# Rotation tables of an SSM on ScalarE, state tiles that stay, and four loads or uses moved by a few slots

## The chip, the cores and the metric

One core of a Trainium2 chip (trn2) runs the kernel. The metric is the device time of one execution in microseconds (us). Its engines: PE (TensorE; PEld is its weight load), DVE (VectorE), ACT (ScalarE), POOL (GpSimd) and SP, which issues most of the DMAs. Each engine takes its instructions in the order of the program, and waits for semaphores set by the others.

## The reference

One layer over x of 4096 rows and 1024 columns, in float32:

```
h    = rmsnorm(x) * pre_g
su, sg, pu, pg, q, k, v, ag = split(h @ W_in)        (widths 256 256 256 256 512 128 128 512)
y_ssm  = GLU(gelu(S5(su) + D*su)) * silu(sg)
y_pool = scale * GroupLinear(meanpool(pu) - pu) * silu(pg)
y_attn = windowed attention(q, k, v, sink) * silu(ag)
x + rmsnorm(concat(y_ssm, y_pool, y_attn) @ W_out) * post_g
```

S5 is a bidirectional complex diagonal recurrence: 16 groups of 16 channels, 64 complex states in each direction, h[t] = lambda * h[t-1] + B u[t], read out by C.

## The kernel before

**Stages.** A matmul in float32 precision is made of three: every operand is held as a high half (rounded by a copy on ScalarE) and a low half (the difference, made on DVE or POOL). The work goes in blocks of 512 rows (8 blocks) and chunks of 128 output columns. Stage 1 projects pool and SSM inputs, normalises x, splits it and stores the split x (`xd`); beside it DVE prepares the SSM's matrices and angle tables, one record of 689 columns for each group (`swd`). Stage 2 projects q, k, v and runs the attention. Stage 3, the gate stage (about 960 to 1300 us), projects the gates sg and ag (`p3_block`), and the 16 SSM groups run beside it (`ssm_group`, lines 1026 to 1110). The output stage multiplies by W_out and finishes.

**The order of the work.** It is written out by a clock of slots (`Slots`, lines 84 to 126): `e.at(slot, fn)` queues a function for a slot, `e.gen` runs a generator, whose `yield n` lets n slots pass, and `e.step()` emits everything that stands in the present slot, in the order in which it was queued there, and goes on to the next. A slot of the gate stage holds 6 projection matmuls, a chunk is four slots. A slot is no time: it fixes only in which order each engine, and SP, gets its instructions. `split(hi, lo, src, eng, lag)` (line 186) copies the high half on ScalarE now and puts the low half on `eng` one slot later.

**One SSM group.** The recurrence over 8 rows at a time is done by matrices, which leaves 512 steps for each group. They are turned into a real recurrence by a rotation: the drive (vr, vi) is multiplied by cos and sin of an angle table, scanned with a real decay rho, and turned back. A group starts every `SSM_PACE` = 8 slots. Its steps, by slot offset: 0 the loads of its record and of u; 4 the split of u (low half on POOL); 6 the angle table `ang`, a sum of two short tables, on POOL; 7 the split of its matrices `w`, and the reduction of the angles to half a turn on DVE (`kt`, `ang`, lines 1045 and 1046); 8 sin and cos on ScalarE (lines 1051 to 1053; cos by Abs and a second Sin); 10 to 12 three products on PE (`mm3`); 13 and 14 the rotation (DVE, and sums on POOL); 15 the split of `wc`; 16 and 17 four scans on DVE with two memsets ahead of each pair (a scan of the state tile's lower 64 partitions runs forward, one of the upper 64 backward); 18 the products that turn the states back: two with S on POOL, two with C on DVE; 20 their sums on POOL; 22 and 23 the splits of `hr` and `hi`; 26 and 27 the last matmuls (lines 1103 and 1105); 28 the copy of the result; 29 its store. So four groups are under way at once, and one engine sees offsets o, o+8, o+16, o+24 of four groups in the same slot.

**What else the change touches.** `p3_open` (line 1000) opens the gate stage: it loads rho, the post gains, the GLU's bias and the GLU's weights, and splits these at once (lag 0, lines 1015 to 1018). The gate chunks are taken out of PSUM on ScalarE, one slot after they are done (`ev_g`, activation in line 1147), and a chunk uses one of two banks. `load_wo` (line 1115) loads a half of a W_out matrix into one of three raw buffers and splits it two slots later. In stage 1, `x_split` (line 260) stores the split x to `xd` (line 279), and `sched_stats` (line 306) computes the row scales of a block two blocks ahead, stores them (`rb_store`) and loads them back, spread over all partitions (`rb_load`, line 335).

## Time and profile before

| | us |
|---|---|
| three runs: median (lowest to highest) | 1708.84 (1708.26 to 1712.75) |
| the profiled execution: its own time | 1709.39 |
| its span, first to last instruction | 1707.6 |
| PE busy in the span | 1592.8 (93%) |
| DVE busy | 1152.2 (67%) |
| ACT busy | 743.1 (44%) |
| POOL busy | 635.4 (37%) |
| mean granted TensorE clock | 0.967 of full speed |

The profile is one execution, read on the core. All times in it count from the start of the span. Matmuls are pipelined, so their busy time is more than the time they occupy PE for: they start 0.23 us apart at full clock and are shown as 0.39 us long. "Idle before" is the time in which an engine had nothing to do ahead of an instruction, with what ended it.

### The profile page before, as it was taken

Reading aid. Unit: us, or ns where it says so; the run is one execution under the profiler, and the core shown is the slowest. Engines: PE = TensorE matmul, PEld = TensorE weight load, DVE = VectorE, ACT = ScalarE, POOL = GpSimd, SP = SyncE. Lnnn points to the kernel's source line nnn. Section 1 sums busy time; section 2 is a strip of 40 time slices with the busy share of each in tenths; the row PEclk is TensorE's granted clock in tenths of the full one; section 3 lists DMA queues with packets and bytes.
Section 4 is the critical chain, followed back from the end, with each engine's and each line's share of the span. In section 5 each row is a group of like instructions: output and inputs, shape, how many; then the busy total and the mean of one; then the engine's idle time right before and its main releaser. Section 6 shows DMA issues by size and latency. Waiting matters only on the chain.

```text
span 1707.6 us, 21061 instructions
## 1 busy us (share of the span) xinstructions
PE 1592.8 (93%) x7364; PEld 1303.7 (76%) x7364; DVE 1152.2 (67%) x2183; ACT 743.1 (44%) x1608; POOL 635.4 (37%) x398
## 2 busy tenths in 40 slices
PE   7997789999999999999999988887889999999998
PEld 5776567778888888888888776666677788888886
DVE  6777768576777777777987378877884745444441
ACT  5323333236666666676776333232333332222221
POOL 0433334341233333333233065565561434334342
PEclk9999899999999999999999999999898999999999
DMA  7597798873221212222333543455358354554532
GB/s 232 183 246 196 195 243 245 315 240 131 87 92 63 69 63 96 83 69 81 119 110 112 200 147 111 159 171 164 104 174 252 121 183 157 164 172 149 163 131 77
DMA packets 121551, 259.07 MB, mean 152 GB/s; under 512 B 31458, under 2 KB 64994, under 8 KB 109668
## 3 DMA queue, kind: packets, MB, share of 16 engines
q1 hardware_dynamic: 115876, 243.03, 45.0%
q10 hardware_dynamic: 5568, 14.68, 2.6%
q8 instruction: 58, 0.95, 0.2%
q14 instruction: 49, 0.40, 0.1%
HBM read 168.93 MB, written 89.80 MB: 152 GB/s over the span
## 4 chain that ended last, share of the span: by engine, by line
PE 45%; DVE 21%; DMA 11%; issue 11%; POOL 9%; ACT 2%; SPq 1%; ACTq 0%; POOLq 0%; DVEq 0%
PE mm L349 5%; PE mm L350 5%; PE mm L351 5%; PE po L894 5%; PE tp L904 5%; PE mm L360 3%; PE o L1260 3%; PE o L1258 3%; PE o L1259 3%; DMA xs<-in_x_dram 3%; PE s L865 3%; PE s L864 3%; POOL ot L161 2%; DMA ga<-agate 2%; DVE xt L164 2%
## 5 line engine op out<-in xcount | busy, mean ns | idle before, releaser
L349 PE MATMUL mm<-xk,w 128*128 128x512 f32 x968 | 391.8, 405 | 8.4 <-ACT gg L1147 6.4
L350 PE MATMUL mm<-xk,w 128*128 128x512 f32 x968 | 386.1, 399 | 0.5 <-DVE xk L164 0.5
L351 PE MATMUL mm<-xk,w 128*128 128x512 f32 x968 | 384.7, 397 | 1.3 <-DVE w L161 1.3
L161 POOL TENSOR_TENSOR ns<-ns,es 128x1536 f32<-128x1536 f32 (+1 forms) x64 | 172.5, 2696 | 403.1 <-ACT pp L172 190.1
L349 PEld LDWEIGHTS mm<-xk,w 128*128 128x128 f32 x968 | 186.3, 192 | 45.4 <-ACT gg L1147 7.4
L351 PEld LDWEIGHTS mm<-xk,w 128*128 128x128 f32 x968 | 185.8, 192 | 43.9 <-DVE w L161 2.9
L350 PEld LDWEIGHTS mm<-xk,w 128*128 128x128 f32 x968 | 186.4, 193 | 35.3 <-DVE xk L164 1.6
L1258 PE MATMUL o<-wo,yk 128*128 128x512 f32 x512 | 201.2, 393 | 3.5 <-ACT gg L1147 3.1
L866 DVE CUSTOM_DVE_ANT_0 ns<-s,cst,nsink 128x384 f32<-128x384 f32 (+1 forms) x256 | 145.8, 607 | 84.6 <-PE s L865 83.4
L1260 PE MATMUL o<-wo,yk 128*128 128x512 f32 x512 | 201.5, 394 | 1.0 <-DVE yk L164 1.0
L1259 PE MATMUL o<-wo,yk 128*128 128x512 f32 x512 | 201.5, 394 | 0.0
L172 ACT ACTIVATE pp<-tp 128x512 fp32r<-128x512 f32 x188 | 112.3, 597 | 170.6 <-PE tp L904 169.6
L360 PE MATMUL mm<-xk,w 128*128 128x512 f32 x552 | 156.4, 422 | 24.3 <-DVE xk L161 14.1
L855 ACT ACTIVATE ns<-ns,nm 128x384 f32<-128x384 f32 (+1 forms) x256 | 152.3, 598 | 2.0 <-DVE nm L866 2.0
L360 PEld LDWEIGHTS mm<-xk,w 128*128 128x128 f32 x552 | 106.1, 200 | 56.0 <-DVE xk L161 18.8
L161 DVE TENSOR_TENSOR pp<-tp,pp 128x512 fp32r<-128x512 f32 x188 | 129.1, 687 | 18.6 <-ACT pp L172 17.2
L894 PE MATMUL po<-pp,vr 128*128 128x512 f32 x376 | 128.2, 422 | 0.0
L904 PE MATMUL tp<-cst,ns 128*128 128x128 f32 x752 | 112.7, 272 | 7.3 <-DVE pp L161 7.3
L904 PEld LDWEIGHTS tp<-cst,ns 128*128 128x128 f32 x752 | 93.1, 140 | 34.4 <-issue 10.1
L1258 PEld LDWEIGHTS o<-wo,yk 128*128 128x128 f32 x512 | 96.5, 189 | 26.3 <-ACT gg L1147 3.5
L1260 PEld LDWEIGHTS o<-wo,yk 128*128 128x128 f32 x512 | 96.6, 189 | 22.6 <-DVE yk L164 1.4
L1259 PEld LDWEIGHTS o<-wo,yk 128*128 128x128 f32 x512 | 96.4, 188 | 21.7
(312 smaller groups left out, 2706.4 us busy)
## 6 DMA issues: line engine op xcount, KB each, us to landing
xk<-xd SPq DMA_DIRECT2D x60, 1024.0 KB
xd<-xk SPq DMA_DIRECT2D x32, 1024.0 KB
xt<-in_xT_dram SPq DMA_DIRECT2D x35, 512.0 KB
xres<-in_x_dram SPq DMA_DIRECT2D x32, 512.0 KB
out_dram<-ot SPq DMA_DIRECT2D x31, 512.0 KB
xs<-in_x_dram ACTq DMA_DIRECT2D x24, 512.0 KB
raw<-in_w_in_dram SPq DMA_DIRECT2D x32, 256.0 KB
yattn<-ysb SPq DMA_DIRECT2D x32, 256.0 KB
```

The source lines that it names most:

```text
L161: return eng.tensor_tensor(out=out, in0=in0, in1=in1, op=op)
L349: T.matmul(o, lhsT=w[:, 0, k], rhs=xh, start=(k == 0), stop=False)
L350: T.matmul(o, lhsT=w[:, 0, k], rhs=xl, start=False, stop=False)
L351: T.matmul(o, lhsT=w[:, 1, k], rhs=xh, start=False, stop=(k == NK - 1))
L360: T.matmul(o, lhsT=w[:, i, k], rhs=XK[b, k][h], start=(n == 0), stop=(n == 3 * NK - 1))
L855: S.activation(out=ns[:, hh, :nk], in_=ns[:, hh, :nk], func=AF.Exp, scale=-1.0, bias=nm[:, hh:hh + 1], accum_out=su[:, hh:hh + 1])
L866: V.tensor_tensor_reduce(out=ns[:, hh, :nk], in0=sp_[:, :nk], in1=cst[:, C_D + c0:C_D + c0 + nk], scale=-(2.0 ** -(h + 1)), scalar=R["nsin ...
L894: T.matmul(po, lhsT=VR[:, (ta + kb) % 8, kv], rhs=pp[:, i], start=(kb == 0 and i == 0), stop=(kb == nkb - 1 and i == 1))
L904: T.transpose(tp[:, hh], ns[:, hh, kb * P:(kb + 1) * P], ident)
L1258: T.matmul(o, lhsT=y[:, 0, ts_], rhs=WO[kk][:, 0, hs], start=first, stop=False)
L1259: T.matmul(o, lhsT=y[:, 0, ts_], rhs=WO[kk][:, 1, hs], start=False, stop=False)
L1260: T.matmul(o, lhsT=y[:, 1, ts_], rhs=WO[kk][:, 0, hs], start=False, stop=last)
```

## The change

Seven edits. (1) In a group, the matrices `w` are split with u at offset 4 and not at 7. (2) The angles are no longer reduced on DVE. At offset 7 four activations make both tables in one tile `cs` of two halves: |a| for the cosine, |a - 1/4| for the sine, then over both halves | |.| - 1/2 |, and one Sin over both; the constant -1/4 gets a column of its own. `ang` moves from offset 6 to 5. (3) The state tiles are two that stay for the whole stage (`gs0`, `gs1`), whose zero columns are written once in `p3_open`. (4) The turning back is one product of both states with C on DVE, over 1024 columns, and one with S on POOL, which is written over the state tile; two sums follow as before. (5) The last matmuls of a group move from offsets 26 and 27 to 28 and 29. (6) The GLU's weights are loaded 30 slots later, one half after the other, each split five slots after its load (low half by one more slot). (7) The split of a W_out half follows its load by 4 slots instead of 2, the store of split x comes 2 slots later, and the load of the row scales 2 slots later.

```diff
--- before.py
+++ after.py
@@ -31,12 +31,11 @@
 CH_SU, CH_SG, CH_PU, CH_PG, CH_Q, CH_K, CH_V, CH_AG = 0, 2, 4, 6, 8, 12, 13, 14
 
 C_ID, C_D, C_E, C_CT, C_INVW, C_EDGE, C_QS = 0, 128, 512, 520, 568, 570, 602
-C_NHALF, C_E1, C_HPI, C_ONE = 606, 614, 742, 743
-NCST = 744
+C_NHALF, C_E1, C_HPI, C_ONE, C_NQ = 606, 614, 742, 743, 744
+NCST = 745
 REC = 689
 TWO_PI = 2.0 * math.pi
 TURN = 6.283185
-RND = 12582912.0
 
 
 def host_constants():
@@ -70,6 +69,7 @@
     c[:, C_E1:C_E1 + 128] = math.e
     c[:, C_HPI] = math.pi / 2
     c[:, C_ONE] = 1.0
+    c[:, C_NQ] = -0.25
     return c
 
 
@@ -276,7 +276,7 @@
             else:
                 tt(V, xk[:, 1, 0], xt[:, 0], f(xk[:, 0, 0]), ALU.subtract)
                 tt(PL, xk[:, 1, 1], xt[:, 1], f(xk[:, 0, 1]), ALU.subtract)
-                e.at(e.now + 6, lambda: dma(out=xd[b % NB, i], in_=f(xk.rearrange("p h j c -> p (h j c)"))))
+                e.at(e.now + 8, lambda: dma(out=xd[b % NB, i], in_=f(xk.rearrange("p h j c -> p (h j c)"))))
             have_x(b, i, xk)
 
         if lag:
@@ -332,7 +332,7 @@
         e.at(d0 + 18, mean, label="p1")
         e.at(d0 + 19, root, label="p1")
         e.at(d0 + 22, rb_store, b, label="p1")
-        e.at(d0 + 28, rb_load, b, label="main")
+        e.at(d0 + 30, rb_load, b, label="main")
 
     def rb_store(s):
         dma(out=rbd[s].rearrange("(j p) -> p j", p=P), in_=rstd[:, 4 * s:4 * s + 4])
@@ -1012,11 +1012,23 @@
         dma(out=glb[:, 0:4], in_=A["glu_b"])
         ts(glb[:, 4:6], glb[:, 2:4], 0.5, ALU.mult)
         gw = cw.tile([P, 2, 2, 4, P], F32R, name="gw")
-        for kk in range(2):
-            raw = wraw.tile([P, 4, P], F32, tag="raw", name="raw")
-            dma(out=raw.rearrange("p m c -> p (m c)"), in_=A["glu_w"][:, kk])
-            split(gw[:, 0, kk], gw[:, 1, kk], raw, V, 0)
-        return dict(ph=ph, sv=sv, gbc=gbc, glb=glb, gw=gw, rho=rho)
+
+        def glu_weights():
+            for kk in range(2):
+                raw = wraw.tile([P, 4, P], F32, tag="raw", name="raw")
+                dma(out=raw.rearrange("p m c -> p (m c)"), in_=A["glu_w"][:, kk])
+                yield 5
+                split(gw[:, 0, kk], gw[:, 1, kk], raw, V)
+
+        e.gen(e.now + 30, glu_weights(), label="main")
+
+        gs = []
+        for n in range(2):
+            gt = sv.tile([P, 2, NC], F32, name=f"gs{n}")
+            V.memset(gt[0:64, :, 0:1], 0.0)
+            V.memset(gt[64:128, :, NC - 1:NC], 0.0)
+            gs.append(gt)
+        return dict(ph=ph, sv=sv, gbc=gbc, glb=glb, gw=gw, rho=rho, gs=gs)
 
     def mm3(o, wh, wl, r, first, last):
         T.matmul(o, lhsT=wh, rhs=r[:, 0], start=first, stop=False)
@@ -1032,26 +1044,24 @@
         yield 4
         ur = sv.tile([P, 2, NC], F32R, tag="ur", name="ur", bufs=2)
         split(ur[:, 0], ur[:, 1], u, PL)
-        yield 2
+        w = sv.tile([P, 2, 3, P], F32R, tag="wb", name="wb", bufs=2)
+        split(w[:, 0], w[:, 1], rec[:, 0:384].rearrange("p (m c) -> p m c", m=3), V)
+        yield 1
+
 
         shc = [P, 16, 32]
         ang = sv.tile(shc, F32, tag="ang", name="ang")
         tt(PL, ang, bc(rec[:, 672:688].unsqueeze(2), shc), bc(rec[:, 640:672].unsqueeze(1), shc), ALU.add)
         rho = bc(R["rho"][:, g:g + 1], [P, NC])
-        yield 1
-        w = sv.tile([P, 2, 3, P], F32R, tag="wb", name="wb", bufs=2)
-        split(w[:, 0], w[:, 1], rec[:, 0:384].rearrange("p (m c) -> p m c", m=3), V)
-        kt = sv.tile(shc, F32, tag="kt", name="kt")
-        ts(kt, ang, RND, ALU.add)
-        stt(ang, kt, RND, ang, ALU.subtract, ALU.subtract)
-        yield 1
-        C_ = sv.tile([P, NC], F32, tag="ct", name="ct", bufs=2)
-        S_ = sv.tile([P, NC], F32, tag="st", name="st", bufs=2)
+        yield 2
+        cs = sv.tile([P, 2, NC], F32, tag="cs", name="cs", bufs=2)
         av = ang.rearrange("p a b -> p (a b)")
-        S.activation(out=S_, in_=av, func=AF.Sin, scale=-TURN)
-        S.activation(out=C_, in_=av, func=AF.Abs)
-        S.activation(out=C_, in_=C_, func=AF.Sin, scale=-TURN, bias=cst[:, C_HPI:C_HPI + 1])
-        yield 2
+        S.activation(out=cs[:, 0], in_=av, func=AF.Abs)
+        S.activation(out=cs[:, 1], in_=av, func=AF.Abs, bias=cst[:, C_NQ:C_NQ + 1])
+        S.activation(out=cs, in_=cs, func=AF.Abs, bias=cst[:, C_NHALF:C_NHALF + 1])
+        S.activation(out=cs, in_=cs, func=AF.Sin, scale=-TURN, bias=cst[:, C_HPI:C_HPI + 1])
+        C_, S_ = cs[:, 0], cs[:, 1]
+        yield 3
         vr = bank(4, [P, NC], "vr")
         mm3(vr, w[:, 0, 0], w[:, 1, 0], ur, True, True)
         yield 1
@@ -1061,45 +1071,39 @@
         o = bank((6, 7, 2, 3)[g % 4], [P, NC], "y")
         mm3(o, w[:, 0, 2], w[:, 1, 2], ur, True, False)
         yield 1
-        wr = sv.tile([P, NC], F32, tag="wr", name="wr", bufs=2)
-        wi = sv.tile([P, NC], F32, tag="wi", name="wi", bufs=2)
-        t2 = sv.tile([P, NC], F32, tag="t2", name="t2")
-        t3 = sv.tile([P, NC], F32, tag="t3", name="t3")
-        tt(V, wr, vr, C_, ALU.mult)
-        tt(V, t2, vi, S_, ALU.mult)
-        yield 1
-        tt(PL, wr, wr, t2, ALU.add)
-        tt(V, wi, vi, C_, ALU.mult)
-        tt(V, t3, vr, S_, ALU.mult)
-        yield 1
-        tt(PL, wi, wi, t3, ALU.subtract)
+        wt = sv.tile([P, 2, NC], F32, tag="wt", name="wt", bufs=2)
+        t2 = sv.tile([P, 2, NC], F32, tag="t2", name="t2")
+        tt(V, wt[:, 0], vr, C_, ALU.mult)
+        tt(V, t2[:, 0], vi, S_, ALU.mult)
+        yield 1
+        tt(PL, wt[:, 0], wt[:, 0], t2[:, 0], ALU.add)
+        tt(V, wt[:, 1], vi, C_, ALU.mult)
+        tt(V, t2[:, 1], vr, S_, ALU.mult)
+        yield 1
+        tt(PL, wt[:, 1], wt[:, 1], t2[:, 1], ALU.subtract)
         wc = sv.tile([P, 2, 2, P], F32R, tag="wc", name="wc", bufs=2)
         split(wc[:, 0], wc[:, 1], rec[:, 384:640].rearrange("p (m c) -> p m c", m=2), V)
         yield 1
-        gr = sv.tile([P, NC], F32, tag="gr", name="gr")
-        gi = sv.tile([P, NC], F32, tag="gi", name="gi")
-        for gt, wt in ((gr, wr), (gi, wi)):
-            V.memset(gt[0:64, 0:1], 0.0)
-            V.memset(gt[64:128, NC - 1:NC], 0.0)
-            V.tensor_tensor_scan(out=gt[0:64, 1:NC], data0=rho[0:64, 0:NC - 1], data1=wt[0:64, 0:NC - 1],
+        gs = R["gs"][g % 2]
+        for i in range(2):
+            V.tensor_tensor_scan(out=gs[0:64, i, 1:NC], data0=rho[0:64, 0:NC - 1], data1=wt[0:64, i, 0:NC - 1],
                                  initial=0.0, op0=ALU.mult, op1=ALU.add)
-            V.tensor_tensor_scan(out=gt[64:128, NC - 2::-1], data0=rho[64:128, 0:NC - 1],
-                                 data1=wt[64:128, NC - 1:0:-1], initial=0.0, op0=ALU.mult, op1=ALU.add)
+            V.tensor_tensor_scan(out=gs[64:128, i, NC - 2::-1], data0=rho[64:128, 0:NC - 1],
+                                 data1=wt[64:128, i, NC - 1:0:-1], initial=0.0, op0=ALU.mult, op1=ALU.add)
             yield 1
-        tt(PL, t2, gi, S_, ALU.mult)
-        tt(PL, wi, gr, S_, ALU.mult)
-        tt(V, wr, gr, C_, ALU.mult)
-        tt(V, t3, gi, C_, ALU.mult)
+        sh2 = [P, 2, NC]
+        tt(V, wt, gs, bc(C_.unsqueeze(1), sh2), ALU.mult)
+        tt(PL, gs, gs, bc(S_.unsqueeze(1), sh2), ALU.mult)
         yield 2
-        tt(PL, wr, wr, t2, ALU.subtract)
-        tt(PL, wi, wi, t3, ALU.add)
+        tt(PL, wt[:, 0], wt[:, 0], gs[:, 1], ALU.subtract)
+        tt(PL, wt[:, 1], wt[:, 1], gs[:, 0], ALU.add)
         yield 2
         hr = sv.tile([P, 2, NC], F32R, tag="hr", name="hr")
-        split(hr[:, 0], hr[:, 1], wr, V)
+        split(hr[:, 0], hr[:, 1], wt[:, 0], V)
         yield 1
         hi = sv.tile([P, 2, NC], F32R, tag="hi", name="hi")
-        split(hi[:, 0], hi[:, 1], wi, V)
-        yield 3
+        split(hi[:, 0], hi[:, 1], wt[:, 1], V)
+        yield 5
         mm3(o, wc[:, 0, 0], wc[:, 1, 0], hr, False, False)
         yield 1
         mm3(o, wc[:, 0, 1], wc[:, 1, 1], hi, False, True)
@@ -1118,7 +1122,7 @@
                 WO[kk] = (WO2[0] if late else wpool).tile([P, 2, DM], F32R, tag="w", name="wo")
             raw = wraw.tile([P, TB], F32, tag="raw", name="rawo")
             dma(out=raw, in_=A["w_out"][kk, :, hf * TB:(hf + 1) * TB])
-            e.at(e.now + 2, prep, hf, raw)
+            e.at(e.now + 4, prep, hf, raw)
 
         def prep(hf, raw):
             hs = slice(hf * TB, (hf + 1) * TB)
```

## Rows read from the trace of the kernel before

**Rows 1.** Table by stages: stretch, length, busy us (xinstructions) by engine, clock, DMA share, GB/s
```profile
1150.00:1200.00 50.00, 40.11 (x153) 31.75 (x152) 40.48 (x56) 16.38 (x31) 28.18 (x22) 0.87 0.47 153
...
1400.00:1500.00 100.00, 100.00 (x437) 81.72 (x436) 47.30 (x59) 27.79 (x53) 41.10 (x29) 1.00 0.50 159
```

**Rows 2.** Timeline of DVE, gate stage: start us, us, engine, line, operation [idle before]
```profile
1003.43 1.47 DVE L168 TENSOR_SCALAR kt<-ang 128x512 f32<-128x512 f32 x1 [1.57 <-POOL ang L161]
...
1144.29 1.22 DVE L1086 TENSOR_TENSOR_SCAN gi<-rho,wi 64x511 f32<-64x511 f32 x1
...
1146.15 1.78 DVE L161 TENSOR_TENSOR t<-gi,ct 128x512 f32<-128x512 f32 x1
...
1153.89 1.47 DVE L168 TENSOR_SCALAR kt<-ang 128x512 f32<-128x512 f32 x1 [1.57 <-POOL ang L161]
...
1158.02 0.68 DVE L161 TENSOR_TENSOR hi<-wi,hi 128x512 fp32r<-128x512 f32 x1
...
1158.98 0.06 DVE L1082 MEMSET gr<- 64x1 f32 x1
...
1163.07 1.22 DVE L1086 TENSOR_TENSOR_SCAN gi<-rho,wi 64x511 f32<-64x511 f32 x1
...
1247.88 1.50 DVE L168 TENSOR_SCALAR kt<-ang 128x512 f32<-128x512 f32 x1 [1.58 <-POOL ang L161]
```

**Rows 3.** Groups of PE, gate stage (960 to 1350 us): busy us, mean ns | idle
```profile
L1023 PE MATMUL y<-hr,wc 128*128 128x512 f32 x16 | 10.2, 635 | 40.4 <-DVE hr L161 40.4
```

**Rows 4.** Timeline of POOL, one period of the gate stage
```profile
1145.65 1.72 POOL L161 TENSOR_TENSOR t<-gi,st 128x512 f32<-128x512 f32 x1 [7.95 <-DVE gi L1086]
...
1149.04 1.29 POOL L161 TENSOR_TENSOR wr<-wr,t 128x512 f32<-128x512 f32 x1
...
1151.55 1.31 POOL L161 TENSOR_TENSOR ur<-u,ur 128x512 fp32r<-128x512 f32 x1
1152.80 1.06 POOL L161 TENSOR_TENSOR ang<-rec 128x512 f32<-128x512 f32 x1
```

**Rows 5.** Groups by line and form, whole span: xcount | busy us, mean ns | idle
```profile
L161 POOL TENSOR_TENSOR ya<-ya,ga 128x1024 f32<-128x1024 f32 x16 | 38.3, 2395 | 72.0 <-DMA ga<-agate 72.0
...
L161 DVE TENSOR_TENSOR q<-q,ys 128x1024 f32<-128x1024 f32 x8 | 9.8, 1225 | 0.3
...
L1210 ACT ACTIVATE q<-q 128x1024 f32<-128x1024 f32 x8 | 8.5, 1059 | 20.0 <-DVE q L161 20.0
```

**Rows 6.** Timeline of ScalarE (ACT), one period of the gate stage
```profile
1151.79 0.62 ACT L172 ACTIVATE hi<-wi 128x512 fp32r<-128x512 f32 x1
...
1157.06 0.63 ACT L1051 ACTIVATE st<-ang 128x512 f32<-128x512 f32 x1 [4.35 <-DVE ang L164]
1157.60 0.61 ACT L1052 ACTIVATE ct<-ang 128x512 f32<-128x512 f32 x1
1158.25 0.72 ACT L1053 ACTIVATE ct<-ct,cst 128x512 f32<-128x512 f32 x1
```

**Rows 7.** Timeline of PE, opening and end of the gate stage
```profile
967.97 0.50 PE L349 MATMUL mm<-xk,w 128*128 128x512 f32 x1 [3.04 <-ACT gg L1147]
...
971.92 0.42 PE L350 MATMUL mm<-xk,w 128*128 128x512 f32 x1
...
1299.44 0.64 PE L1258 MATMUL o<-wo,yk 128*128 128x512 f32 x1 [3.11 <-ACT gg L1147]
```

**Rows 8.** Chain that ended last, opening of the gate stage: start us, us, what
```profile
960.83 4.52 DMA raw<-in_glu_w_dram
...
973.44 9.30 DMA u<-udram
```

**Rows 9.** Waits of SP's queue, first stage (0 to 440 us): us in total, times, longest
```profile
SPq L279 <- DVE xk L161: 57.0, 13, 11.6
...
SPq L343 <- DMA rbd<-rstd: 35.1, 5, 10.0
```

**Rows 10.** Waits of the engines, first stage (40 to 440 us)
```profile
DVE xt L164 <- DMA rb<-rbd: 10.5, 4, 4.5
```

## The prediction

> **What bounds the kernel now.** The shares of busy time mislead here, so the first view is the table by stages [rows 1]: in the output stage PE issues 437 matmuls in 100 us (0.229 us each, clock 1.00); in the gate stage, where the SSM groups run beside it, only 153 in 50 us, at a granted clock of 0.87. A group comes every eight slots: 48 projection matmuls and its own 15, so PE needs 63 x 0.229 = 14.4 us for it. But the tables of successive groups are reduced on DVE at 1003.43 and, thirteen periods later, at 1247.88 [rows 2]: 18.80 us each. So 4.4 us of every period are lost on PE, and they show as its wait for the low half of hr, 40.4 us in sum [rows 3], and as the lowered clock behind it.
>
> What makes 18.80 us is a loop over DVE and POOL, read from the two timelines. The last scan of a group ends at 1144.29 + 1.22 = 1145.51 [rows 2]. POOL then does two sine products from 1145.65 to 1149.04, two sums to 1151.55, the low half of the next u to 1152.80 and the next angle table to 1153.86 [rows 4]. Only then can DVE reduce that table (from 1153.89), write low halves until 1158.98, and scan until 1163.07 + 1.22 = 1164.29 [rows 2]. Every step follows the one before: 18.78 us. A change is worth what it takes out of this loop, times the 14 passes that carry a table (groups 2 to 15).
>
> **The loop after the change.** The diff takes the reduction (1.47 us and the operation behind it) and four memsets off DVE, and makes one wide product of two on either engine. But with the new offsets written modulo eight, two orders follow. First, POOL's sine product now overwrites the state tile, so it waits for DVE's cosine product, where both ran side by side before. Second, the four table activations stand at offset 7 and are queued on ScalarE ahead of the high half of hi (offset 23) and of wc (offset 15); DVE's low halves of hi and wc stand ahead of the next scans. So the table of the group after next is still in the loop, now through ScalarE. From the end of the last scan:
>
> - DVE's cosine product over 1024 columns, 0.03 + 1.22 for the same shape [rows 5], then 0.14 to POOL (1145.51 to 1145.65 [rows 2, 4]).
> - POOL's product over 1024 columns: 2.40 [rows 5]. Beside DVE operations with two SBUF inputs POOL loses time: its two products of 512 took 3.39, where two sums take 2.51 [rows 4]; that is 0.88 for DVE's two cosine products of 512 columns, of which one shows 1.78 us [rows 2]; 0.43 each. Now the low half of wb (384 columns) falls beside it: 0.33.
> - Two sums 2.51, u's low half 1.25, angles 1.06 [rows 4]; hr's low half falls beside them: 0.43.
> - ScalarE, 0.03 later. The first Abs, 0.54 to the next (as from 1157.06 to 1157.60); the second with a bias operand, 0.72 + 0.04, as the third reads it; the third and fourth, over 1024 columns with a bias, 1.15 each (1.06 [rows 5] plus the 0.1 by which the biased Sin at 1158.25 exceeds the Abs at 1157.60 [rows 6]), less some 0.07 of net overlap before the next: 3.53 for the four.
> - High half of hi 0.62 [rows 6], 0.03, DVE's low halves of hi and wc 0.96 (1158.02 to 1158.98), four scans 4 x 1.22 = 4.9 without the memsets [rows 2].
>
> Sum: 1.25 + 0.14 + 2.73 + 5.25 + 0.03 + 3.53 + 0.65 + 0.96 + 4.9 = 19.44 us against 18.80: +0.64 a pass, **+9.0 us** over 14. The ends: with no loss on POOL and no wait between activations it is 18.4 (-0.4 a pass, -6); with POOL's wide product at the disturbed price of the old pair, 3.39, it is 20.1 (+1.3, +18). I take the middle, where each piece has a row of its own kind.
>
> On the activations a page and a row differ. The row: the Abs at 1157.60 lasts 0.61 and the Sin that reads its result starts 0.65 later, so a dependent pair does not overlap [rows 6]. The Trainium skill ("ScalarE: Activation LUTs", section "What ACT_TABLE_LOAD costs") lets back-to-back activations overlap by about 93 ns and gives 186 or 280 ns plus 0.833 ns a column; an estimate by it for the four is 3.2 us, by which the sum would be some 4.5 us lower. I go by the row.
>
> Off the loop: the products from PSUM now come before any wait for POOL's sums; 1.25 us and some five operations of about 0.65 into the pass they are done, and POOL wants them at 9. The split of wb with a group's inputs has its data: u and its record are fetched when wc's low half has freed the old record, five us ahead. The last SSM matmuls go two slots later, which changes where PE waits, not how long. The cover of all this is the 4 us by which the loop exceeds PE's work. PE's wait will stand at a chunk's bank, to be emptied by the gate activation (L1147) that is queued behind hr's high half, and no more at hr's low half.
>
> **The opening of the stage.** Now the GLU weights are issued ahead of group 0's inputs and split at once on ScalarE: the gate activation behind that ends late, PE waits 3.04 us for it and then takes 3.95 us until 971.92 for ten matmuls that take 2.3 at full clock [rows 7]. This delay is on the chain: PE frees xk tiles, SP loads them, and only behind that is group 1's u issued, at 973.44, to take 9.30 us [rows 8]. With the weights later these 3.0 + 1.7 go, and u moves with them: **-4.7 us**; between 0 (u lands as late for the traffic) and -6 (0.5 MB less ahead of it). What the weights cost later: two transfers with five slots to land, past which SP has only work that waits for data anyway; two activations in ScalarE's idle time; two low halves on DVE, one in the loop (0.6), one beside POOL (0.43): **+1.0**, between 0 and 2.
>
> **The tail.** The w_out halves wait two slots longer before they are split, so the last gate activation stands behind one split and not behind two that wait for their transfers. PE's wait there is 3.11 us [rows 7], and by the opening's row another 1.6 at low clock; a bank must still be emptied, about 0.7. I take **-3.5**, between 0 (three raw buffers, now held longer, make the transfers late instead) and -4.7.
>
> **The first stage.** Row scales are loaded, and split x stored, two slots later; on SP one x load passes ahead of both. SP today sits 35.1 us in the scale loads until the scale store has landed, and 57.0 us in the stores of x for their data [rows 9]; so the scale loads go out no later than now, and the stores have no reader for a stage. DVE waits 10.5 us in all for scales [rows 10]. I cost this at nothing; SP's own wait is the cover. The ends are -10.5 and, if seven loads came two slots (12 matmuls, 2.7 us) later without cover, +19; being nearest to SP's 35.1 I keep within about 4 of nothing.
>
> **Sum:** +9.0 + 1.0 - 4.7 - 3.5 = +1.8 on the profiled execution's 1709.39, which lies 0.55 above the median 1708.84: **1710.6 us** against 1708.84. A measurement here tells 0.3% (5.1 us) from no change, so the forecast is no change.
>
> **Rivals.**
> 1. *The loop gets a little shorter:* POOL isn't disturbed and activations overlap. For it: POOL's sums, beside products from PSUM, show no loss. Against it: the disturbed rows. -6 in place of +9: 1696.
> 2. *The tables leave the loop:* if ScalarE did hi and wc ahead of the tables, the loop would close through POOL's two sums of the next group, near 15.5 us, -3.3 a pass: about 1655. Against it: the same reading of the slots gives every order seen in rows 2, 4 and 6.
> 3. *Slower, by POOL's wide product:* at the 3.39 us of the disturbed pair the pass is 20.1 and the sum +18 + 1 - 8.2: 1719. It decides from about 3.1 us for that product upward.
> 4. *The ends bring nothing:* u of group 1 lands as before and PE's two waits only move; +9 + 1: 1719 too.
> 5. *The first stage gains:* with an x load ahead of the scale load DVE waits less; the whole 10.5 us gives 1700.
>
> **Chances.** Forecast (1703.7 to 1714) 0.43; rival 1 0.17, rival 2 0.05, rival 5 0.08: faster 0.30; rival 3 0.17 and rival 4 0.10: slower 0.27. The range takes in rivals 1, 3, 4 and 5 and leaves out rival 2 and the far ends of the first stage: 1696 to 1720.
>
> **What would show it.** Right: the angle tables of POOL follow at 19.2 to 19.7 us; its wide product takes 2.6 to 2.8; hi's high half starts on ScalarE right behind the Sin of 1024 columns; DVE idles some 5 us before hi's low half; PE waits on L1147 instead of hr; no wait near 965, and less than 1.5 us at the end of the gate stage. Wrong: a period under 18.5 or over 20, hi's high half ahead of the tables, PE at clock 1.00 throughout, or a first stage that is longer or shorter by more than 4 us.

## The result and the profile after

Four runs of the changed kernel take 1729.76 us in the median (1727.34 to 1735.34), the kernel before 1709.78 beside them: ratio **1.0119 [1.0091, 1.0148]**, slower by 20 us, where 1710.6 was forecast with 1720 as the upper end. The profiled execution has a span of 1725.6 us against 1707.6, so there are 18.0 us to find. Three marks part them: the load of the sink's row at the end of the first stage, the angle tables of groups 0, 1 and 15 on POOL, and the end.

The first mark, SP's timeline of the kernel before and then of the changed one (start us, us):

```profile
386.23 0.33 SPq L832 DMA_DIRECT2D sink<-in_sink_dram  x1
```

```profile
401.32 0.33 SPq L832 DMA_DIRECT2D sink<-in_sink_dram  x1
```

The others, POOL's timeline of the kernel before, and then of the changed one with one pass of the loop in full:

```profile
972.46 1.05 POOL L161 TENSOR_TENSOR ang<-rec 128x512 f32<-128x512 f32 x1
984.72 1.05 POOL L161 TENSOR_TENSOR ang<-rec 128x512 f32<-128x512 f32 x1
...
1246.79 1.06 POOL L161 TENSOR_TENSOR ang<-rec 128x512 f32<-128x512 f32 x1
```

```profile
988.37 1.37 POOL L161 TENSOR_TENSOR ang<-rec 128x512 f32<-128x512 f32 x1
...
997.03 1.36 POOL L161 TENSOR_TENSOR ang<-rec 128x512 f32<-128x512 f32 x1
...
1164.88 2.38 POOL L161 TENSOR_TENSOR gs<-gs,cs 128x1024 f32<-128x1024 f32 x1 [8.95 <-DVE wt L161]
1167.33 2.69 POOL L161 TENSOR_TENSOR wt<-wt,gs 128x512 f32<-128x512 f32 x2
1169.99 1.83 POOL L161 TENSOR_TENSOR ur<-u,ur 128x512 fp32r<-128x512 f32 x1
1171.77 1.05 POOL L161 TENSOR_TENSOR ang<-rec 128x512 f32<-128x512 f32 x1
...
1184.27 2.35 POOL L161 TENSOR_TENSOR gs<-gs,cs 128x1024 f32<-128x1024 f32 x1 [8.94 <-DVE wt L161]
...
1203.61 2.63 POOL L161 TENSOR_TENSOR gs<-gs,cs 128x1024 f32<-128x1024 f32 x1 [8.94 <-DVE wt L161]
...
1268.66 1.05 POOL L161 TENSOR_TENSOR ang<-rec 128x512 f32<-128x512 f32 x1
```

These are the tables of groups 0, 1 and 15. So the way to group 0 is 15.9 us longer, from group 0 to 1 3.6 shorter, from 1 to 15 9.6 longer (19.40 a pass for 18.72), and from there to the end (456.9 for 460.8) 3.9 shorter: 15.9 - 3.6 + 9.6 - 3.9 = 18.0. At the sink's load 15.1 of the 15.9 are there already: **the loss is the first stage**.

The loop runs as the forecast had it. ScalarE's timeline of that pass [rows 6]:

```profile
1172.85 0.63 ACT L1059 ACTIVATE cs<-ang 128x512 f32<-128x512 f32 x1 [2.42 <-POOL ang L161]
1173.39 0.71 ACT L1060 ACTIVATE cs<-ang,cst 128x512 f32<-128x512 f32 x1
1174.13 1.15 ACT L1061 ACTIVATE cs<-cs,cst 128x1024 f32<-128x1024 f32 x1
1175.32 1.15 ACT L1062 ACTIVATE cs<-cs,cst 128x1024 f32<-128x1024 f32 x1
1176.38 0.61 ACT L172 ACTIVATE hi<-wt 128x512 fp32r<-128x512 f32 x1
```

From the first Abs to hi are 3.53 us, the figure of the sum. DVE's timeline behind it [rows 2]:

```profile
1177.08 0.69 DVE L161 TENSOR_TENSOR hi<-wt,hi 128x512 fp32r<-128x512 f32 x1 [6.42 <-issue]
...
1182.96 1.22 DVE L161 TENSOR_TENSOR wt<-gs,cs 128x1024 f32<-128x1024 f32 x1
1184.50 2.53 DVE L161 TENSOR_TENSOR wb<-rec,wb 128x384 fp32r<-128x384 f32 x1 [0.31 <-ACT wb L172]
...
1203.45 0.55 DVE L161 TENSOR_TENSOR wb<-rec,wb 128x384 fp32r<-128x384 f32 x1
```

DVE waits 6.42 us for hi, scans for 4.9 and POOL's next product starts at 1184.27: the loop closes through ScalarE. The waits of PE, 950 to 1290 us (total, times, longest), name the gate activation now and hr no more [rows 3]:

```profile
PE mm L349 <- ACT gg L1151: 31.9, 9, 4.6
```

In the first stage three things show. The waits for scales, 40 to 440 us, were 10.5 [rows 10]:

```profile
DVE xt L164 <- DMA rb<-rbd: 27.8, 5, 9.6
```

And SP's timeline, before and then after, from one scale store (rbd<-rstd) to the scale load (rb<-rbd) that reads it:

```profile
100.18 0.37 SPq L338 DMA_DIRECT2D rbd<-rstd  x1
...
104.48 0.32 SPq L279 DMA_DIRECT2D xd<-xk  x1
111.62 0.32 SPq L343 DMA_DIRECT2D rb<-rbd  x1
...
113.26 6.56 SPq L734 DMA_DIRECT2D udram<-su  x2
```

```profile
99.69 0.37 SPq L338 DMA_DIRECT2D rbd<-rstd  x1
...
103.89 0.60 SPq L734 DMA_DIRECT2D udram<-su  x1
104.60 9.68 SPq L279 DMA_DIRECT2D xd<-xk  x1
114.49 0.55 SPq L734 DMA_DIRECT2D udram<-su  x1
115.60 4.16 SPq L343 DMA_DIRECT2D rb<-rbd  x1
```

The scale load used to be the next thing out once the store had landed. Now both u stores (L734) have come in front of it, and the issue of the x store between them alone lasts 9.68 us.

ScalarE, which issues its own loads of x rows (L317), stands longer ahead of three of them. Below is the operation behind each of these loads, with the idle time that ends when the load is out, before and then after: 26.4 us in sum, and 38.7.

```profile
164.36 0.60 ACT L172 ACTIVATE e<-mm 128x512 f32<-128x512 f32 x1 [2.86 <-DMA ypool<-yp]
208.54 0.60 ACT L172 ACTIVATE stg<-pst 128x512 f32<-128x512 f32 x1 [9.96 <-DMA rbd<-rstd]
256.68 0.60 ACT L172 ACTIVATE e<-mm 128x512 f32<-128x512 f32 x1 [13.61 <-DMA swd<-tab]
```

```profile
169.71 0.60 ACT L172 ACTIVATE e<-mm 128x512 f32<-128x512 f32 x1 [7.02 <-DMA xt<-in_xT_dram]
220.19 0.60 ACT L172 ACTIVATE stg<-pst 128x512 f32<-128x512 f32 x1 [15.85 <-PE mm L351]
267.65 0.60 ACT L172 ACTIVATE e<-mm 128x512 f32<-128x512 f32 x1 [15.79 <-DMA swd<-tab]
```

Why a load of x waits for transfers that it has no use for is told under "Later x stores".

### The profile page after: what moved, and what is told of

Same layout as the page of the kernel before. It is cut to its first block, busy times and chain, and to the rows that moved or that the text cites. A ratio compares the mean times of both kernels' runs of the same rounds, so it can differ in the third digit from the quotient of the medians.

```text
span 1725.6 us, 20895 instructions
## 1 busy us (share of the span) xinstructions
PE 1590.7 (92%) x7364; PEld 1301.7 (75%) x7364; DVE 1102.9 (64%) x2075; ACT 769.9 (45%) x1624; POOL 629.3 (36%) x382
## 4 chain that ended last, share of the span: by engine, by line
PE 48%; DVE 17%; DMA 12%; POOL 11%; issue 6%; ACT 3%; SPq 1%; POOLq 0%; ACTq 0%; DVEq 0%
PE mm L349 5%; PE mm L350 5%; PE mm L351 5%; PE po L894 5%; PE tp L904 5%; PE o L1264 4%; PE o L1263 4%; PE o L1262 4%; POOL wt L161 3%; DMA xt<-in_xT_dram 3%; PE mm L360 3%; PE s L865 3%; PE s L864 3%; POOL gs L161 2%; DVE xt L164 2%
## 5 line engine op out<-in xcount | busy, mean ns | idle before, releaser
L161 DVE TENSOR_TENSOR pp<-tp,pp 128x512 fp32r<-128x512 f32 x188 | 129.2, 688 | 18.6 <-ACT pp L172 17.2
L1263 PEld LDWEIGHTS o<-wo,yk 128*128 128x128 f32 x512 | 96.1, 188 | 21.5
```

The lines of the kernel that those rows point to most:

```text
L161: return eng.tensor_tensor(out=out, in0=in0, in1=in1, op=op)
L1263: T.matmul(o, lhsT=y[:, 0, ts_], rhs=WO[kk][:, 1, hs], start=False, stop=False)
```

## The experiments

All ratios are to the kernel before in the same set of runs. The chips differ (before takes 1709.7, 1709.9, 1707.4, 1703.1 and 1702.8 us in the five sets), so ratios are compared, or times within a set. The times in the expectations are written for a kernel before of some 1709.8 us; where it took less, the ratio is held against them.

**Which edit.** First each of the two edits of the first stage alone.

```diff
# e1_rb28: the changed kernel, scale load as before
-        e.at(d0 + 30, rb_load, b, label="main")
+        e.at(d0 + 28, rb_load, b, label="main")
# e2_xd6: the changed kernel, x store as before
-                e.at(e.now + 8, lambda: dma(out=xd[
+                e.at(e.now + 6, lambda: dma(out=xd[
# e3_before_rb30: the kernel before with the late scale load only
-        e.at(d0 + 28, rb_load, b, label="main")
+        e.at(d0 + 30, rb_load, b, label="main")
```

> The changed kernel with one edit undone: the load of the row scales is back at its old slot (28 instead of 30). Theory A (the scale load now stands behind the store of u, whose two DMAs are made of pieces of 512 bytes, on SP's queue): the first stage is back to its old length, DVE waits about 10 us for scales instead of 27.8, the sink load (line 832) goes out near 386 us instead of 401, and what is left is the rest of the forecast, 1709 to 1716 us. Theory B (the later store of split x is what lengthens the first stage): still 1722 or more. Theory C (neither; the other edits lengthen it through traffic): still 1722 or more and nothing moves in the next run either.

> The changed kernel with the other edit of the first stage undone: the store of split x is back at its old slot (6 instead of 8), the scale load stays late. Theory A: the store has no reader, so the time stays within 4 us of the changed kernel, 1724 to 1734, with DVE's wait for scales still over 20 us. Theory B: 1709 to 1716.

> The old kernel with this one edit alone: the scale load two slots later. Theory A: 12 to 17 us slower than before, 1721 to 1727, all of it ahead of 410 us; DVE's wait for scales above 20 us. Theory B: 1706 to 1712, no change.

Measured: 1728.00, 1.0108 [1.0088, 1.0127]; 1731.17, 1.0124 [1.0105, 1.0144]; 1726.58, 1.0108 [1.0082, 1.0135]. The second and third came as their theory A had them. The first did not: with the scale loads back, the loss is there all the same, as its theories B and C said. Either edit alone costs what both cost, so both have to be undone:

> The changed kernel with both edits of the first stage undone (scale load back at slot +28, split-x store back at +6); the rest of the change stands. Theory A (the excess is in the first stage alone, and either edit alone suffices to cost some 16 us of it, since undoing only one left 1728.0 and 1731.2): first stage as before, the load of the attention's sink at 386 to 388 us, loop +9.6, opening and tail -3.6 and -3.9: 1709 to 1714, ratio 0.999 to 1.003. Rival B (a later stage carries part of the excess, and the first stage only moved): 1718 to 1728.

Measured: **1709.95, 0.9998 [0.9989, 1.0007]** (both lines above changed back). That is the forecast's own time, so the two edits of the first stage are the whole loss. The mark moves with them too. Six traces have the first stage as before, with the same instructions in the same order, and the sink's load goes out there at 379.05 to 389.17 us (before 386.23, f1_both 384.76); in the eight traces with either edit whole and nothing else put later it goes out at 400.5 to 404.5. The ten microseconds within the first lot are the spread between chips and executions, and smaller shifts of this mark in one trace show nothing.

**Later scale loads.** In the kernel before with only that edit, the waits of DVE (40 to 440 us) and SP's timeline:

```profile
DVE xt L164 <- DMA rb<-rbd: 52.6, 5, 16.4
```

```profile
101.86 0.37 SPq L338 DMA_DIRECT2D rbd<-rstd  x1
...
113.77 7.55 SPq L734 DMA_DIRECT2D udram<-su  x2
121.36 2.99 SPq L343 DMA_DIRECT2D rb<-rbd  x1
```

19.5 us pass from store to load, before 11.4. Two runs take away what stands between:

```diff
# g3_rb_first: scale load at +30, x store at +6
-            e.at(e.now + 3, decay_store, c_r, c_i, gs)
+            e.at(e.now + 4, decay_store, c_r, c_i, gs)
-                    e.gen(e.now + 4, su_dmas(s))
+                    e.gen(e.now + 6, su_dmas(s))
# h4_all_behind: decay stores at +5 and u stores at +6, and the x store
+                e.at(e.now + 10, lambda: dma(out=xd[
```

> The changed kernel with the split-x store back at +6 and the scale load left at +30 (1731.2), and the u stores at +6 in place of +4 and the decay stores at +4 in place of +3, so that on SP the scale load stands ahead of both again. Theory A (behind these stores the scale load goes out 8 to 10 us later, and VectorE's wait for scales grew from 10.5 to 52.2 us): that wait falls under 20 us and the time to 1709 to 1717. Rival B (two slots later is what costs, whatever stands ahead): wait above 40 us, 1724 to 1733.

> The changed kernel with the scale load left at +30, and the split-x stores at +10, the u stores at +6 and the decay stores at +5, so that none of these three stands between the landing of a scale store and the scale load on SP; ScalarE's loads are not held by a scale store but once. Theory A (it is the stores ahead of it on SP that make the scale load late): VectorE's wait for scales under 20 us, 1708 to 1718. Rival B (two x loads that now stand ahead of it, or two slots by themselves): wait of 30 us and more, 1719 to 1730.

Measured: 1.0069 [1.0052, 1.0087] (1720.35) and 1.0059 [1.0044, 1.0074] (1713.08); DVE's wait for scales falls from 52.2 us to 39.5 and 16.3. So moving the u and decay stores behind the scale load takes away about half of the loss of 1.0124. g3_rb_first lies between its two theories in wait and in time. Its trace shows where the rest stays: the scale load of block 4 goes out 13.6 us after its store, for 12.6 in the kernel before, but DVE's operation that waits for it starts 12.6 us behind the issue (167.78 to 180.36) for 5.7 (162.97 to 168.67). What makes the load land later is open. With the x stores behind as well, in h4_all_behind, the wait is 16.3 us for the old 10.5, as theory A had it; by the ratio the time is in rival B's range, and x stores that late have a price of their own, which comes next.

**Later x stores.** With them alone SP's order is not much worse and DVE's wait for scales is down to 4.2 us. What the trace shows is on ScalarE, in e1_rb28:

```profile
163.27 0.37 ACTq L317 DMA_DIRECT2D xs<-in_x_dram  x1
163.75 1.13 ACT L172 ACTIVATE k<-kp 16x512 f32<-16x512 f32 x2 [13.00 <-DMA rbd<-rstd]
```

ScalarE loads the rows of x for the statistics itself (L317), and here it stands 13 us until a scale store has landed that it has no use for. The built program says why. Its transfers share eight completion counters, and one that is given a counter waits until the transfer that had it has landed. (The trace has the same: eight semaphores for the 551 transfers; the scale store signals number 108, the load of x rows is told to wait for 108, which the store last raises at 163.25, and goes out at 163.27.) The instructions of e1_rb28, on SP and on ScalarE (DMAHW with its figure is the counter; the scale store, row 65, is given number 6):

```
65 L338 DMA rbd<-rstd 128x4x1 [waits DMAHW6_49,Pool_49]
69 L343 DMA rb<-rbd 128x512 [waits DMAHW6_49,DMAHW2_49]
100 L317 DMA xs<-in_x_dram 128x1024 [waits DMAHW6_49]
```

The scale load waits for it as its reader, the load of x rows only as the next owner of the counter. With the x store at +8 and the scale load at +28 that happens in two of six blocks (4 and 6). The first two attempts to show that this is the cause failed:

```diff
# f2_spare: x store at +8, scale load at +28; behind every scale store
+        for _ in range(2):
+            dma(out=spare[s], in_=cst[:, 0:4])
# g1_after: the same, behind the stores of blocks 4 and 6 alone; g2_ahead: ahead of them
+        for i_ in range({4: 2, 6: 2}.get(s, 0)):
+            dma(out=spare[3 * s + i_], in_=A["glu_b"][:, 0:4])
```

> The changed kernel with the scale load back at +28, the split-x store left at +8, and behind each of the six scale stores two spare stores of 128x4 elements to a scratch tensor that nobody reads: work is added. The built program hands its DMAs eight completion counters in turn, and a DMA whose counter is still held by an earlier one waits for that one to land. With the x store at +8 the counter of the scale store (which takes 12 us to land) falls to ScalarE's next load of x rows in two of the six blocks (trace: ScalarE idle 13.0 us until the scale store has landed); the two spare stores move it to x loads and scale loads on SP. Theory A (counters): the 16 to 18 us over the version with both edits undone go, 1709 to 1717, no wait of ScalarE for a scale store. Rival B (the x store stands ahead of an x load on SP, and that order is what costs): 1726 to 1733, as without the spare stores.

> As the run with the scale load back at +28 and the split-x store left at +8 (1728.0), with two spare loads of 128x4 elements from an input into tiles nobody reads, right behind the scale stores of blocks 4 and 6 alone: 4 transfers are added in all. (The spare stores of the run before this wrote one place twice, so the second waited 63.2 us in sum for the first and the run told nothing of counters.) In the built program these loads move the counters of the two scale stores from ScalarE's next load of x rows, four DMAs behind, to x loads on SP nine DMAs behind; all else that those loads wait for stays. Theory A (counters): ScalarE's wait of 13.0 us for a scale store is gone, block 5's scale store comes 7 to 9 us sooner, and the time is 1708 to 1718. Rival B (the order of x store and x load on SP): 1725 to 1731.

> The control of the run before: the same four spare loads, but right ahead of the scale stores of blocks 4 and 6, so that the counters of both scale stores still fall to ScalarE's next load of x rows. Theory A (counters): no gain, 1726 to 1732, ScalarE waits 12 to 14 us for a scale store. Rival C (any added transfer shifts the stage by as much, or the gain of the other run is by chance): as the other run, within 3 us.

Measured: 1.0134, 1.0123 and 1.0123 (1732.74, 1728.69, 1729.45). In the first the second spare store writes what the first writes and so waits for it: SP stood 63.2 us for it, and the run says nothing of counters. In g1_after the counter did pass on, but ScalarE waits as long for its new holder:

```profile
163.19 1.14 ACT L173 ACTIVATE k<-kp 16x512 f32<-16x512 f32 x2 [13.29 <-DMA spare<-in_glu_b_dram]
```

A small load issued right behind the scale store, on the same queue, lands no sooner than it. So the wait was never taken away, and both runs agree with either theory. Next the counter was moved by the choice of the x stores that go late, and the wait was also put in by hand:

```diff
# h1_x012: scale load at +28; h2_x123 has (1, 2, 3)
+                e.at(e.now + (8 if i in (0, 1, 2) else 6), lambda: dma(out=xd[
# h3_hold: both edits undone, and in the load of x rows
+            if j == 0 and b in (5, 7):
+                S.dma_start(out=held[b], in_=rbd[b - 1:b, 0:4])
```

> The changed kernel with the scale load back at +28 and three of the four split-x stores of a block (first, second, third) at +8, the fourth back at +6. In the built program no scale store of blocks 4 and 6 hands its counter to ScalarE's next load of x rows any more (an x store and a pool store, both issued ahead of the scale store, do). (The spare loads of the run before were issued right behind the scale store on the same queue and landed no sooner, so ScalarE waited 13.3 us for a spare load in place of 13.0 us for the scale store: the wait was not taken away.) Theory A (ScalarE's two holds until the scale store has landed are the loss of the later x stores): no hold of ScalarE over 9 us before its loads of blocks 5 and 7, 1708 to 1716. Rival B (x stores later are dearer by themselves, in proportion): three quarters of 18 us, 1721 to 1727.

> The twin of the run before: scale load at +28, and the second, third and fourth split-x store at +8, the first back at +6. In the built program both scale stores still hand their counters to ScalarE's next load of x rows. Theory A (holds): 1725 to 1731, ScalarE waits 12 to 14 us for a scale store. Rival B (in proportion): as the twin, within 3 us.

> The version with both edits of the first stage undone (1709.95), with the suspected wait put in by hand: ahead of the first load of x rows of blocks 5 and 7, ScalarE's queue loads four elements of the scales just stored (of blocks 4 and 6) into a tile nobody reads, so it stands until that store has landed. No x store is later than before. Theory A (the two holds are the whole loss): 1722 to 1730. Rival B (ScalarE has the time; the loss is elsewhere): 1709 to 1714.

Measured: 1711.38, 1.0050 [1.0035, 1.0065]; 1719.89, 1.0102 [1.0085, 1.0119]; 1718.89, 1.0093 [1.0078, 1.0108]. ScalarE's timeline at the place in question, in this order (added lines move the line numbers by up to three):

```profile
148.89 0.43 ACTq L317 DMA_DIRECT2D xs<-in_x_dram  x1
```

```profile
160.60 1.13 ACT L172 ACTIVATE k<-kp 16x512 f32<-16x512 f32 x2 [11.50 <-DMA rbd<-rstd]
```

```profile
161.70 1.13 ACT L173 ACTIVATE k<-kp 16x512 f32<-16x512 f32 x2 [13.36 <-DMA held<-rbd]
```

The first row is the load itself, which goes out at once; in the others ScalarE stands 11.50 and 13.36 us. By their ratios the second and third are in theory A's ranges, and the first lies between its two theories. The twins move the same number of stores, and the one that holds ScalarE is 8.5 us slower. That is what the holds cost, as far as it doesn't matter which three of the four stores go late. To see what the unheld twin loses, it was run beside the version with both edits undone:

> The version with both edits of the first stage undone, once more, now on one chip with the version that has three x stores at +8 and no hold. Both theories: within 0.15% of before (0.9998 in its first run).

> The version with the first three x stores at +8 and no hold of ScalarE, beside the version with all of them at +6 on the same chip. Its first ratio was 1.0050 on a chip where the kernel before took 1703.12, but its trace has the load of the sink at 382.74 us, no later than with all stores at +6 (384.76). Theory A (the holds are the whole loss): within 4 us of that version. Rival B (later x stores cost some 8 us besides the holds): 7 to 10 us above it.

Measured: 1704.15, 1.0010 [1.0002, 1.0019], and 1713.09, 1.0055 [1.0041, 1.0069]. The wait put in by hand takes 1718.89 - 1704.15 = 14.7 us (0.4 of it is the other set's chip), and only the two small loads were added there, which also move the counters of the transfers behind them: holding ScalarE at two places is enough for most of the loss. But three late x stores without these holds still cost 8.9 us, so "the holds are the whole loss" is refuted. What the 8.9 are is open. The traces offer ScalarE's idle time at the three loads of x rows shown for the kernel before: 4.91, 14.97 and 13.75 us in i2_x012_again for 1.31, 10.03 and 11.35 in i1_both_again, the middle one behind an x store that had the counter. But f1_both, the same program as the second, has 4.18, 9.84 and 13.47, and taking these waits away was not tried.

In the changed kernel itself the scale loads are later too, and the counters fall otherwise: no load of x rows waits there for a scale store. The three waits of 7.02, 15.85 and 15.79 us are for a load of x, an x store and the store of an angle table that had the counter before. So these runs show that such holds cost time; how the changed kernel's 20 us part between them and DVE's longer waits for scales, they don't show.

**The ends.**

```diff
# g4_ends_back: both edits of the first stage undone, and
-            e.at(e.now + 4, prep, hf, raw)
+            e.at(e.now + 2, prep, hf, raw)
# and the GLU weights loaded and split at once, as before
```

> The version with both edits of the first stage undone (1709.95), and also the GLU weights loaded early and split at once, and the w_out halves split two slots after their load, as before: what is left of the change is the tables, the state tiles and the split with a group's inputs. Theory A (the prediction's terms for the opening, -4.7 + 1.0, and the tail, -3.5; in the trace of the changed kernel -3.6 and -3.9): 7 to 8 us more, 1716 to 1719. Rival B (the ends bring nothing, u lands as late either way): 1708 to 1712.

Measured: 1717.15, 1.0044 [1.0027, 1.0060], against 0.9998: 7.9 us, in theory A's range, with some 3 us of noise by the two intervals. The trace doesn't put them where the theory does. Against f1_both the span is 6.5 us longer (1715.3 for 1708.8), and 4.4 of it stand at the sink's load already, where both run the same instructions. From group 0 to group 1 it is 1.8 longer, and PE's wait for the gate activation is there again (2.74 us at 970.41; no wait over 1 us near it in f1_both): that is the opening. From group 15 to the end it is 0.9 longer (458.7 for 457.8), less than the spread of this stretch in the fourteen traces that have the late split and the tables at offset 7 (456.9 to 459.4). So the opening's gain is shown, at about 2 us, and the tail's is not: of the 3.9 us by which the changed kernel's tail is shorter, g4_ends_back has 2.1 without the later split.

**The tables out of the loop.**

```diff
# e4_tables8: scale load at +28; f3_t8_both: both edits undone; in the group, activations at offset 8
-        yield 2
+        yield 3
         cs = sv.tile([P, 2, NC], F32, tag="cs", name="cs", bufs=2)
...
-        yield 3
+        yield 2
# f4_sums_first: f3_t8_both with u's split, w's split and ang at offset 8, activations at 9
-        yield 4
+        yield 8
         ur = sv.tile([P, 2, NC], F32R, tag="ur", name="ur", bufs=2)
```

> As the first of these runs, and the four table activations one slot later (offset 8 instead of 7), so that ScalarE takes the high halves of hi and wc ahead of them; nothing else moves. Theory of the forecast (the tables hold the loop at 19.4 us a pass only because they are queued ahead of hi and wc): the pass closes through POOL's two sums of the next group, 15.5 to 16.2 us; 14 passes save 45 to 54 us against the first run, 1657 to 1670. Rival (the pass is set by POOL's work and by DVE's operations beside it, wherever the tables stand): over 18.5 us a pass, no more than 12 us saved.

> The changed kernel with both edits of the first stage undone and the four table activations one offset later (8 in place of 7), so that ScalarE does the high halves of hi and wc ahead of them. Theory A (the two are independent): pass of 17.2 us as in the run with the tables at 8 (18.8 before), first stage as before: 1677 to 1683, ratio 0.980 to 0.986. Rival B (the shorter first stage is paid back in the gate stage's opening): 1688 to 1697.

> As the version with both edits undone and the tables one offset later, and with the low half of u and the angles at offset 8 in place of 4 and 5 (activations at 9), so that GpSimd does the two sums of the next group ahead of them. Theory A (with the tables at 8 the loop of 17.2 us runs over GpSimd: product 2.7, two sums 2.5, low half of u 1.7, angles 1.5, two sums 2.7, then 6.1 of scans and the cosine product; low half and angles now leave it): 14 us over GpSimd, so TensorE's 14.4 us of matmuls bound the pass at 14.4 to 15.5 and the time is 25 to 39 us below that version: 1640 to 1656. Rival B (a wait of TensorE for ScalarE's bank-emptying behind the tables, or the lowered clock, holds the pass at 16.5 us and more): 1667 to 1680.

Measured: 1696.72, 0.9920 [0.9897, 0.9943]; **1677.12, 0.9810 [0.9795, 0.9824]**; **1675.07, 0.9795 [0.9778, 0.9811]**. One slot takes the pass from 19.4 to 17.2 us, not to the 15.5 named, and the time of e4_tables8 is in neither range. f3_t8_both is in theory A's range, f4_sums_first in rival B's and no faster than f3_t8_both beyond the noise. POOL's timeline of e4_tables8:

```profile
1163.38 2.65 POOL L161 TENSOR_TENSOR gs<-gs,cs 128x1024 f32<-128x1024 f32 x1 [6.11 <-DVE wt L161]
1166.11 2.49 POOL L161 TENSOR_TENSOR wt<-wt,gs 128x512 f32<-128x512 f32 x2
1168.55 1.74 POOL L161 TENSOR_TENSOR ur<-u,ur 128x512 fp32r<-128x512 f32 x1
1170.26 1.49 POOL L161 TENSOR_TENSOR ang<-rec 128x512 f32<-128x512 f32 x1
1171.71 2.74 POOL L161 TENSOR_TENSOR wt<-wt,t 128x512 f32<-128x512 f32 x2
```

The loop now closes over POOL: product, two sums, u's low half, the angles and the next group's two sums follow without a gap, then POOL stands for 6.11 us until DVE's scans, which start behind the first of those sums, and the cosine product are done. In f4_sums_first the low half and the angles stand behind those sums, and the pass is still 17.15 us. DVE's timeline there, and then PE's:

```profile
1150.53 1.51 DVE L161 TENSOR_TENSOR wc<-rec,wc 128x256 fp32r<-128x256 f32 x1
1151.96 2.06 DVE L1086 TENSOR_TENSOR_SCAN gs<-rho,wt 64x511 f32<-64x511 f32 x1
```

```profile
1155.15 0.50 PE L1035 MATMUL vr<-ur,wb 128*128 128x512 f32 x1 [1.04 <-POOL ur L161]
1156.82 0.57 PE L1036 MATMUL vr<-ur,wb 128*128 128x512 f32 x1 [1.18 <-DVE wb L161]
```

wc's low half takes 1.51 us and two scans 2.06 and 2.13, for 0.42 and 1.22 in the changed kernel: they run beside the POOL work that was moved. u's low half now stands last on POOL and wb's behind the two slow scans on DVE, and PE waits for both; it has no other idle time over 0.3 us in this pass. Behind these waits the granted clock is 0.54 (the 1.2 GHz level) from 1156.80 to 1160.40, and matmuls start 0.43 us apart where 0.23 is usual. The chain that the profile follows through this pass runs over DVE (wc, two scans, wb), then 9.0 us over PE, then over ScalarE back to hi and wc. So the lowered clock and a wait of PE hold the pass, as rival B had it, though the wait is for low halves and not for a bank. My expectation of 14.4 to 15.5 us missed that. How much each part costs was not separated.

## Why the prediction was wrong

- **The loop: right.** 19.44 us a pass were forecast, 19.40 came. Two of the passes (19.76 and 19.92, the others 19.3 to 19.4 but for a first of 18.9) hold the GLU's splits, +0.9 in sum for the +1.0. Together 10.0 were forecast and 9.6 came. Of the terms, ScalarE's four activations hit their 3.53 exactly; POOL's wide product took 2.45 to the next start for 2.73 (over the stage 2.35 to 2.77, so the sign "2.6 to 2.8" came in part), and its sums, low half and angles 5.49 (from 1167.33 to the end of the angles at 1171.77 + 1.05) for 5.25. The estimate of 3.2 us for the activations, by the rates of the Trainium skill ("ScalarE: Activation LUTs", section "What ACT_TABLE_LOAD costs"), was too low: the pairs that depend on each other start 0.74 and 1.19 us apart, longer than the first of each lasts.
- **Opening and tail: the sum came, its parts are not shown.** The stretches are 3.6 and 3.9 us shorter in the trace, for -4.7 and -3.5, and the run that undoes both edits is 7.9 us slower, for 7.2 with the weights' price. But its trace gives the opening about 2 us and the tail nothing clear of its spread, so part of the agreement is luck: the tail without the later split is 2.1 us shorter too (458.7 for 460.8), for which the prediction has no term.
- **The first stage: the step that failed.** Its term was put at nothing and measured 1.0119 - 0.9998, some 20.7 us. It reads: "on SP one x load passes ahead of both ... so the scale loads go out no later than now, and the stores have no reader for a stage ... SP's own wait is the cover." Three things were wrong in it. SP's wait of 35.1 us covers only transfers that are queued behind it, and within the two slots the u and decay stores come out too and go ahead of the scale load; these were not counted. A wait at the head of a queue is cover only as long as nothing gets in between. Second, a store without a reader is not free: moving it changed which transfer ScalarE's load of x rows has to see landed first. Third, the range: the far end of +19 was worked out, and then narrowed to "about 4" on the strength of that same cover. Either edit alone lost 16.9 to 21.5 us.
- **A sign of it was in the trace.** The waits of ScalarE in the first stage of the kernel before have a row that names a scale store, of which ScalarE reads nothing: the 9.96 us at 208.54, shown above.
- **The rivals.** POOL's product never came near 3.1 (rival 3); the loop got longer and not shorter (rival 1); the ends brought something, if not each what it should (rival 4); the first stage moved the other way (rival 5). Rival 2 was out by its condition, but the one-slot run shows it was worth 33 us (f3_t8_both against f1_both), at 17.2 us a pass and not near 15.5: u's low half and the angles stay in POOL's chain.

With both edits of the first stage undone, the change is no change, 0.9998, as the sum of the other four terms says, the loop's by its own mechanism, the tail's not.

## What to carry to other kernels

When a transfer is moved by some slots, list everything that every other generator issues on that queue within them, and price the wait that its reader will then have; a wait at the head of the queue covers only what stays behind it. A wait whose releaser shares no data with the waiting instruction points to a shared completion counter: any change of the order of transfers deals these out anew, so a slow small store should be followed by transfers that can wait (a piece of advice that no run here tested: the spare loads landed too late for it). And when one step leaves a loop, write down what closes it next before pricing the gain: here it was ScalarE, then POOL, then a chain over DVE, PE and ScalarE, at 19.4, 17.2 and 17.15 us.

## What the runs showed of the hardware

- A low half on DVE (384 columns, two inputs in SBUF) takes 2.53 us when it starts 0.23 us after POOL's product: it ends 0.41 after POOL's instruction does (1184.27 + 2.35), while POOL's own 2.35 is no longer than the 2.40 of the same shape in [rows 5]. One pass later it starts 0.16 us ahead of the product (1203.45 and 1203.61) and takes 0.55, and the product is the one that takes longer, 2.63. The forecast had charged POOL 0.33 for it in every pass. The Trainium skill ("SBUF — State Buffer", section "SBUF: two separate sides") says that whichever of the two starts first gets the shared pair of ports for its whole instruction; the rows of both passes agree.
- A scale store of 512 elements takes 11.4 us until its reader may go (100.18 to 111.62), and a load of 2 kB issued right behind it lands no sooner: ScalarE's 13.29 us in g1_after, for 13.00 behind the store itself. The Trainium skill ("DMA: Bandwidth & Descriptors", section "Queues, rings and completion order") has the completion of a transfer land only after every earlier write from the same DMA engine; the run agrees with it.
- The issue of one transfer held SP for up to 9.68 us behind a u store; in the first 440 us of the kernel before three quarters of SP's issues last 0.55 us or less, and the longest 5.43.
